# Attention and its output products: a written order of turnings, scores and half products on all engines, in place of the planner's

## The chip, the cores and the metric

The kernel runs on one core of a Trainium2 chip. The metric is the device time of one execution in microseconds. The engines are named as in the profile: PE (TensorE, matrix products; its weight loads are PEld), DVE (VectorE), ACT (ScalarE), POOL (GpSimd), and SP (SyncE), which issues the DMAs.

## The reference

One layer of a diffusion backbone for 512 latent tokens (width 1024) and 256 context tokens: a half-step SwiGLU FFN, token mixing, a second half-step SwiGLU FFN, all in float32. The part at issue is the token mixing and where the second FFN begins.

```
def one_block(q_blk):                       # 128 queries, 8 heads, 512 + 256 keys
    s = einsum('bqhd,bkhd->bhqk', q_blk, k_all) * scale
    p = softmax(s, axis=-1)
    return einsum('bhqk,bkhd->bqhd', p, v_all)

attn = block_attention(q, k_all, v_all)     # 8 heads of 64
sg   = chunk_gmlp(u, v, ...)                # 8 groups of 64
x    = x + mx[5] * (concatenate([attn, sg]) @ w_out)
x    = ffn_sublayer(x, mx[6], mx[7], mx[8], norm3_w, ffn2_w1, ffn2_w3, ffn2_w2)
```

## The kernel before, in words

**Arithmetic.** Every large product is done as three matmuls: each operand is split into a high part, rounded to the matmul's format, and a low part, the remainder (`mm3`, line 165: high·high, low·high, high·low). Making a pair takes a copy on ACT and a subtraction on DVE; `Stream.split` (line 138) does it for weights, in halves of 512 columns, after `Stream.half` has loaded a weight unit of 128 x 1024 by an SP DMA.

**Attention** (lines 1484 to 1606) has 8 heads and 4 blocks of 128 queries, so 32 steps (h, t).

- `qk_head` (1487) turns a head's queries (4 turnings) and keys (2 x 3 turnings) by matmuls with the identity, and splits them into qth, qtl, kth, ktl.
- `scores` (1509): 6 matmuls of 128 x 384 into a two-bank tile `big`, of which there are two; DVE takes the row maximum mx (1519), ACT the exponential pe with its row sum sm (1520), DVE the reciprocal (1521), and POOL scales pe (1522).
- `probs_t` (1525) turns the 6 blocks of pe in two banks `mm` of three, of which there are four; ACT copies the high part pth (1539), DVE subtracts the low part ptl (1540). The second bank of every odd block goes another way: ACT copies it to pf (1535), and POOL makes both parts (1536, 1537).
- `pv` (1542): for two blocks together, 12 matmuls of 128 x 256 by the values vv, then ol on ACT (1551), oc on DVE (1552), and the pair mixh on ACT and mixl on POOL (1554, 1555), which the output products read.
- `out_mm` (1557): output products of one 128-wide tile of the model dimension. The gate's half of w_out is multiplied ahead of and between the first scores, in 8 tiles of 12 matmuls of 128 x 512; the attention's half needs mixh and mixl, and is done for token half 0 and then half 1, in tiles of 12 matmuls of 128 x 256 each.

The step loop (1586) puts scores three steps ahead of the turnings (`LOOK`), and the four weight units of the attention's half (uo0 to uo3) at steps 4, 7, 10 and 13.

**What sets the order.** Engines run their own instructions in order. In this part `nc.ordered` is False (from line 1322): the program's order is only a hint, and a planner that works with estimated durations decides each engine's order. `Core` (62) hands out engines: with `nc.ordered = True` vector, scalar and gpsimd are wrapped in `Pinned` (51), which keeps their instructions in program order; with "all", tensor too. From line 1661 the order is pinned by True.

**After the attention.** `out_mms` (1643) and `out_evs` (1649) do the attention's half: matmuls, the addition into x on DVE, and squares of x on ACT. The sums of squares over the tiles, sqa, are added on DVE by `SsqAcc.flush` (403), one object for each token half, sA and sB (1657), which are handed `nc.vector` when they are made, before line 1661. `done` (425) sums over partitions by a matmul with ones and derives rstd on DVE (rv). `h3` (1627) then forms the second FFN's normed input, hfA into the blocks b11 and b21, hfB into b12 and b22. The second FFN starts with plain products (`plain`: 48 matmuls of 128 x 256 for two weight units and one token half) and goes on with a Winograd scheme from about 845 us on.

## Time and profile before

| | |
|---|---|
| median of 3 runs | 1152.52 us (1152.01 to 1155.87) |
| profiled execution: its own time | 1152.95 us |
| profiled execution: span of the trace | 1151.2 us |
| mean granted TensorE clock | 0.999 |
| busy: PE, DVE, ACT, POOL | 1132.2, 910.8, 534.2, 319.3 us |
| first turning of a query | 670.52 us |
| first output product of token half 1 | 782.19 us |

The profile is of one execution. A row of a timeline gives the start in us from the span's start, the duration, the engine, the line, the operation, output <- inputs by the program's names, shapes, and a count where several alike follow one another; in brackets stands how long the engine stood idle before it and what it waited for. Matmuls overlap in the array, so the distance of two starts, not the duration, is what one costs. Windows give the engines' busy time in a stretch.

### The profile page before, as it was taken

Reading aid. Unit: us, or ns where it says so; the run is one execution under the profiler, and the core shown is the slowest. Engines: PE = TensorE matmul, PEld = TensorE weight load, DVE = VectorE, ACT = ScalarE, POOL = GpSimd, SP = SyncE. Lnnn points to the kernel's source line nnn. Section 1 sums busy time; section 2 is a strip of 40 time slices with the busy share of each in tenths; the row PEclk is TensorE's granted clock in tenths of the full one; section 3 lists DMA queues with packets and bytes.
Section 4 is the critical chain, followed back from the end, with each engine's and each line's share of the span. In section 5 each row is a group of like instructions: output and inputs, shape, how many; then the busy total and the mean of one; then the engine's idle time right before and its main releaser. Section 6 shows DMA issues by size and latency. Waiting matters only on the chain. (4 is left out here: it accounts for less than half of the span.)

```text
span 1151.2 us, 18763 instructions
## 1 busy us (share of the span) xinstructions
PE 1132.2 (98%) x7084; PEld 1071.9 (93%) x7084; DVE 910.8 (79%) x1687; ACT 534.2 (46%) x1085; POOL 319.3 (28%) x277
## 2 busy tenths in 40 slices
PE   8999999999999999999999999999999999999998
PEld 6799999999999999999988788999999989898997
DVE  6978989888888788867647979869876969686884
ACT  5555421431344214445735448976543535353451
POOL 0002302311333023200027536760013425152330
PEclk9999999999999999999999999999999999999999
DMA  9530253244334664322343101002121422233312
GB/s 343 187 131 19 92 190 117 102 160 147 116 126 146 235 201 166 110 69 64 100 137 102 55 19 58 18 1 92 56 93 56 145 76 93 91 111 110 111 38 92
DMA packets 35674, 125.89 MB, mean 109 GB/s; under 512 B 3712, under 2 KB 10624, under 8 KB 30976
## 3 DMA queue, kind: packets, MB, share of 16 engines
q1 hardware_dynamic: 35440, 124.63, 31.6%
q8 instruction: 56, 0.92, 0.3%
q14 instruction: 34, 0.28, 0.1%
q10 hardware_dynamic: 144, 0.06, 0.0%
HBM read 122.58 MB, written 2.10 MB: 108 GB/s over the span
## 5 line engine op out<-in xcount | busy, mean ns | idle before, releaser
L59 POOL TENSOR_TENSOR block<-block 128x512 f32<-128x512 f32 x69 | 105.0, 1522 | 395.2 <-DVE opl L59 392.5
L59 DVE TENSOR_TENSOR opl<-block,oph 128x512 fp32r<-128x512 f32 x216 | 183.1, 854 | 32.5 <-ACT oph L59 30.2
L59 ACT CAST oph<-block 128x512 fp32r<-128x512 f32 x216 | 133.8, 621 | 142.3 <-PE mm L59 93.5
L59 PE MATMUL mm<-gh,oph 128*128 128x384 f32 (+1 forms) x440 | 155.2, 353 | 0.0
L59 PE MATMUL mm<-gl,oph 128*128 128x384 f32 (+1 forms) x440 | 154.9, 352 | 0.0
L59 PE MATMUL mm<-gh,opl 128*128 128x384 f32 (+1 forms) x440 | 154.9, 352 | 0.0
L59 DVE SCALAR_TENSOR_TENSOR x<-mm,g,x 128x256 f32<-128x256 f32 (+2 forms) x184 | 83.0, 489 | 48.9 <-PE mm L59 48.2
L59 ACT CAST oph<-raw 128x512 fp32r<-128x512 f32 x105 | 63.8, 619 | 88.7 <-PE mm L59 66.7
L59 POOL TENSOR_TENSOR block<-s,block 128x512 f32<-128x512 f32 x35 | 47.1, 1347 | 150.9 <-DVE opl L59 150.3
L59 PEld LDWEIGHTS mm<-gh,opl 128*128 128x128 f32 x440 | 82.6, 188 | 5.7
L59 PEld LDWEIGHTS mm<-gh,oph 128*128 128x128 f32 x440 | 82.6, 188 | 5.6
L59 PEld LDWEIGHTS mm<-gl,oph 128*128 128x128 f32 x440 | 82.6, 188 | 5.5
L59 DVE TENSOR_TENSOR opl<-raw,oph 128x512 fp32r<-128x512 f32 x105 | 70.4, 684 | 9.2 <-ACT oph L59 8.7
L59 PE MATMUL mm<-hh,oph 128*128 128x384 f32 x192 | 64.5, 336 | 0.0
L59 PE MATMUL mm<-hl,oph 128*128 128x384 f32 x192 | 64.2, 334 | 0.0
L59 PE MATMUL mm<-hh,opl 128*128 128x384 f32 x192 | 64.1, 334 | 0.0
L59 DVE SCALAR_TENSOR_TENSOR junk<-raw,cb 128x1024 bf16<-128x1024 f32 x48 | 62.2, 1309 | 0.0
L59 POOL TENSOR_TENSOR s<-block 128x512 f32<-128x512 f32 x34 | 50.5, 1486 | 18.9 <-DMA block<-wst 18.9
L59 PE MATMUL one<-hh,oph 128*128 128x384 f32 x144 | 48.1, 334 | 0.0
L59 PE MATMUL one<-hl,oph 128*128 128x384 f32 x144 | 48.1, 334 | 0.0
L59 PE MATMUL one<-hh,opl 128*128 128x384 f32 x144 | 48.1, 334 | 0.0
L59 DVE SCALAR_TENSOR_TENSOR raw<-raw,cb 128x1024 f32<-128x1024 f32 x32 | 42.1, 1323 | 6.2 <-DMA raw<-wada 6.1
(662 smaller groups left out, 3471.1 us busy)
## 6 DMA issues: line engine op xcount, KB each, us to landing
raw<-wst SPq DMA_DIRECT2D x77, 512.0 KB, 3.7
block<-wst SPq DMA_DIRECT2D x36, 1024.0 KB, 4.9
raw<-wada SPq DMA_DIRECT2D x56, 512.0 KB, 4.0
scale<-wada SPq DMA_DIRECT2D x8, 512.0 KB, 7.6
shift<-wada SPq DMA_DIRECT2D x8, 512.0 KB, 7.4
x<-xT SPq DMA_DIRECT2D x5, 512.0 KB, 6.7
raw<-wfirst SPq DMA_DIRECT2D x8, 256.0 KB, 7.1
out<-x SPq DMA_DIRECT2D x7, 256.0 KB, 2.3
```

The lines of the kernel that those rows point to most:

```text
L59: return lambda *a, **k: self.tc.keep_in_program_order(f(*a, **k))
```

## The change

Only the attention's part is rewritten, and one line behind it. The amount of arithmetic stays the same: the same matmuls, splits and loads.

- After the third weight unit of the gate's half, `nc.ordered = "all"`: the order of all four compute engines is the program's from here to the head of the second FFN, where True follows as before.
- Four banks are taken once and kept: A0 and A1 for turnings of probabilities (TB), Q0 for a piece of a head, P0 for the products by values. The scores keep the two tiles `big`.
- A step i = 3 to 31 is written out: maximum of step i−1, reciprocal and scaling of step i−2, the 6 turnings of step i−3, one piece of the next head (queries, keys, keys, none), the evacuation of a product by values, the high and low parts of the turnings, exponential of step i−1, 6 scores of step i, and 6 of the 12 matmuls of a product by values.
- The first two steps' scores stand between the last tiles of the gate's half. The halves of the weights uo1 to uo3 come one by one: the high half at the end of steps 6, 10, 14, 18, 22, 26, its low half ("late") in the next step behind the maximum. The two halves of uo0 come before step 3, the second one between the exponential of step 1 and the maximum of step 2.
- At the end the first four output tiles of token half 0 stand between the last turnings and products by values, their fourth heads' pair last.
- sA and sB are now made while `nc.ordered` is "all", so the `nc.vector` that they keep is the one that pins.

The core of the diff:

```diff
+    og2 = st.unit(U_OG + 2)
+    nc.ordered = "all"
+    A0, A1, Q0, P0 = (mm() for _ in range(4))
+    TB = A0, A1
...
+    s_mm(1)
+    s_mm(2)
+    s_norm(0)
...
+    uo_half(0)()
+    evac_lat(A0, 7, 1)
+    s_max(1)
+    s_exp(1)
+    uo_half(1)()
+    late = None
+    for i in range(3, LAST):
+        j = i - 3
+        if i in (3, 4, 11):
+            raw_uo.append(st.half(wst, U_OA + len(raw_uo)))
+        s_max(i - 1)
+        if late:
+            late()
+            late = None
+        s_norm(i - 2)
+        t_mm(j, TB)
+        piece = (i // 4 + 1, i % 4) if i % 4 < 3 and i // 4 + 1 < HEADS else None
+        if piece:
+            qk_mm(*piece, Q0)
+        p = (i - 7) // 2
+        if i >= 7 and i % 2:
+            pv_out(p, P0)
+        for a in range(2):
+            t_hi(j, a, TB[a])
+            t_lo(j, a, TB[a])
+        if piece:
+            qk_hi(*piece, Q0)
+            qk_lo(*piece, Q0)
+        s_exp(i - 1)
+        if i >= 7 and i % 2:
+            pv_mix(p, nc.gpsimd)
+        if i in (6, 10, 14, 18, 22, 26):
+            late = uo_half(i // 4 + 1)
+        s_mm(i)
+        if i >= 5:
+            pv_mm((i - 5) // 2, range(3) if i % 2 else range(3, 6), P0)
...
     for q in range(4):
-        out_evs(0, sA, q, out_mms(0, q))
+        out_evs(0, sA, q, early[q] if q < 2 else out_mms(0, q))
```

Here `uo_half(n)` does the high half at once and returns the low half as a function; `s_norm` is the reciprocal and POOL's scaling, `t_mm` the turnings, `t_hi` and `t_lo` their two parts, `pv_mm` and `pv_out` the product by values and its evacuation, `pv_mix` the pair for the output products.

More of the change, by code (lines that the diff above doesn't have):

```diff
@@ L1485, in layer_kernel @@
     ip = ictx.enter_context(tc.tile_pool(name="ip", bufs=2))
-    def qk_head(h):
-        qth = ip.tile([QH, 512], F32R, tag="qth", name=f"qth{h}")
-        qtl = ip.tile([QH, 512], F32R, tag="qtl", name=f"qtl{h}")
-        kth = ip.tile([QH, 768], F32R, tag="kth", name=f"kth{h}")
-        ktl = ip.tile([QH, 768], F32R, tag="ktl", name=f"ktl{h}")
-        pt = mm()
-        for t in range(4):
-            nc.tensor.transpose(pt[:QH, t * P : t * P + P], qn[:, t, h, :], ident)
-        w = wqk[:QH, 0:1]
-        nc.scalar.activation(qth, pt[:QH], AF.Copy, scale=w)
-        nc.vector.scalar_tensor_tensor(qtl, pt[:QH], w, qth.bitcast(F32), ALU.mult, ALU.subtract)
-        for a in range(2):
-            pb = mm()
-            for t in range(3):
-                nc.tensor.transpose(pb[:QH, t * P : t * P + P], kn[:, 3 * a + t, h, :], ident)
-            c = slice(384 * a, 384 * a + 384)
-            nc.scalar.copy(kth[:, c], pb[:QH, :384])
-            nc.vector.tensor_sub(ktl[:, c], pb[:QH, :384], kth[:, c].bitcast(F32))
-        return qth, qtl, kth, ktl
@@ L1507, in layer_kernel, with qk_mm @@
-    last_out = []
-    def scores(h, t, tiles):
-        qth, qtl, kth, ktl = tiles
-        pb = big()
+    heads, pes, pts, sms, ols = {}, {}, {}, {}, {}
+    steps = [(h, t) for h in range(HEADS) for t in range(4)]
+    LAST = len(steps)
+    def qk_mm(h, n, pt):
+        if n == 0:
+            heads[h] = [ip.tile([QH, c], F32R, tag=f"{s}t{p}", name=f"{s}t{p}{h}") for s, c in (("q", 512), ("k", 768)) for p in "hl"]
+            for t in range(4):
+                nc.tensor.transpose(pt[:QH, t * P : t * P + P], qn[:, t, h, :], ident)
+        else:
+            for t in range(3):
+                nc.tensor.transpose(pt[:QH, t * P : t * P + P], kn[:, 3 * n - 3 + t, h, :], ident)
@@ new lines, in qk_hi, with qk_lo @@
+    def qk_hi(h, n, pt):
+        if n == 0:
+            nc.scalar.activation(heads[h][0], pt[:QH], AF.Copy, scale=wqk[:QH, 0:1])
+        else:
+            nc.scalar.copy(heads[h][2][:, 384 * n - 384 : 384 * n], pt[:QH, :384])
+    def qk_lo(h, n, pt):
+        th, tl = heads[h][:2] if n == 0 else [t[:, 384 * n - 384 : 384 * n] for t in heads[h][2:]]
+        if n == 0:
+            nc.vector.scalar_tensor_tensor(tl, pt[:QH], wqk[:QH, 0:1], th.bitcast(F32), ALU.mult, ALU.subtract)
+        else:
+            nc.vector.tensor_sub(tl, pt[:QH, :384], th.bitcast(F32))
@@ L1512, in scores, with s_mm @@
+    def s_mm(i):
+        h, t = steps[i]
+        qth, qtl, kth, ktl = heads[h]
+        pb = sms[i] = big()
         s = slice(t * P, t * P + P)
@@ L1515, in scores, with s_max @@
             mm3(nc, pb[:, n, :384], (qth[:, s], qtl[:, s]), (kth[:, m], ktl[:, m]), True, True)
-        mx = ip.tile([P, 1], F32, tag="mx", bufs=4, name=f"mx{h}{t}")
-        sm = ip.tile([P, 1], F32, tag="sm", bufs=4, name=f"sm{h}{t}")
-        pe = ip.tile([P, 768], F32, tag="pe", bufs=4, name=f"pe{h}{t}")
+    def s_max(i):
+        pb = sms[i]
+        mx = ip.tile([P, 1], F32, tag="mx", bufs=4, name=f"mx{i}")
         nc.vector.tensor_reduce(mx, pb[:, :, :384], axis=AX.XY, op=ALU.max, negate=True)
+        sms[i] = pb, mx
@@ L1520, in scores, with s_exp, s_norm, by_pool @@
+    def s_exp(i):
+        pb, mx = sms.pop(i)
+        sm = ip.tile([P, 1], F32, tag="sm", bufs=4, name=f"sm{i}")
+        pe = ip.tile([P, 768], F32, tag="pe", bufs=4, name=f"pe{i}")
         nc.scalar.activation(pe.rearrange("p (a c) -> p a c", a=2), pb[:, :, :384], AF.Exp, bias=mx, accum_out=sm)
+        pes[i] = pe, sm
+    def s_norm(i):
+        pe, sm = pes[i]
         nc.vector.reciprocal(sm, sm)
         nc.gpsimd.tensor_scalar(pe, pe, sm, 0.0, ALU.mult, ALU.add)
-        return pe
-    def probs_t(pe, pth, ptl, c0):
-        c = slice(c0, c0 + P)
+    def by_pool(j, a):
+        return j % 2 == 1 and a == 1 and j < LAST - 4
@@ L1527, in probs_t, with t_mm @@
+    def t_mm(j, banks):
+        pe = pes.pop(j)[0]
+        if j % 2 == 0:
+            pts[j // 2] = [ip.tile([P, 6, 256], F32R, tag=f"pt{p}", name=f"pt{p}{j}") for p in "hl"]
         for a in range(2):
-            pq = mm()
             for i in range(3):
-                nc.tensor.transpose(pq[:, i * P : i * P + P], pe[:, (3 * a + i) * P : (3 * a + i) * P + P], ident)
-            src = pq[:, :384].rearrange("p (k c) -> p k c", c=P)
-            b = slice(3 * a, 3 * a + 3)
-            if c0 and a:
-                pf = ip.tile([P, 3, P], F32, tag="pf", bufs=1, name=f"pf_{nc.next_id()}")
-                nc.scalar.copy(pf, src)
-                nc.gpsimd.tensor_scalar(pth[:, b, c], pf, 1.0, 0.0, ALU.mult, ALU.add)
-                nc.gpsimd.tensor_sub(ptl[:, b, c], pf, pth[:, b, c].bitcast(F32))
-                continue
@@ L1539, in probs_t @@
-            nc.scalar.copy(pth[:, b, c], src)
-            nc.vector.tensor_sub(ptl[:, b, c], src, pth[:, b, c].bitcast(F32))
-    def pv(h, half, pth, ptl):
-        pt = mm()
-        for t in range(6):
-            nc.tensor.matmul(pt[:, :256], vv[:, t, h, :], pth[:, t, :], start=t == 0, stop=False)
-            nc.tensor.matmul(pt[:, :256], vv[:, t, h, :], ptl[:, t, :], start=False, stop=t == 5)
-        r = slice((h % 2) * 64, (h % 2) * 64 + 64)
-        c = slice(half * 256, half * 256 + 256)
-        oc = ip.tile([P, 256], F32, tag="oc", name=f"oc{h}{half}")
-        ol = ip.tile([P, 256], F32, tag="ol", bufs=1, name=f"ol{h}{half}")
+                nc.tensor.transpose(banks[a][:, i * P : i * P + P], pe[:, (3 * a + i) * P : (3 * a + i) * P + P], ident)
@@ new lines, in t_parts, with t_hi @@
+    def t_parts(j, a, bank):
+        c, b = slice(j % 2 * P, j % 2 * P + P), slice(3 * a, 3 * a + 3)
+        return bank[:, :384].rearrange("p (k c) -> p k c", c=P), [t[:, b, c] for t in pts[j // 2]]
+    def t_hi(j, a, bank):
+        src, (th, tl) = t_parts(j, a, bank)
+        if by_pool(j, a):
+            pf = ip.tile([P, 3, P], F32, tag="pf", bufs=1, name=f"pf_{j}")
+            nc.scalar.copy(pf, src)
+            nc.gpsimd.tensor_scalar(th, pf, 1.0, 0.0, ALU.mult, ALU.add)
+            nc.gpsimd.tensor_sub(tl, pf, th.bitcast(F32))
+        else:
+            nc.scalar.copy(th, src)
@@ new lines, in t_lo, with pv_mm, pv_out @@
+    def t_lo(j, a, bank):
+        if not by_pool(j, a):
+            src, (th, tl) = t_parts(j, a, bank)
+            nc.vector.tensor_sub(tl, src, th.bitcast(F32))
+    def pv_mm(p, ts, pt):
+        th, tl = pts[p]
+        for t in ts:
+            nc.tensor.matmul(pt[:, :256], vv[:, t, p // 2, :], th[:, t, :], start=t == 0, stop=False)
+            nc.tensor.matmul(pt[:, :256], vv[:, t, p // 2, :], tl[:, t, :], start=False, stop=t == 5)
+        if t == 5:
+            pts.pop(p)
+    def pv_out(p, pt):
+        r = slice((p // 2 % 2) * 64, (p // 2 % 2) * 64 + 64)
+        oc = ip.tile([P, 256], F32, tag="oc", name=f"oc{p}")
+        ol = ip.tile([P, 256], F32, tag="ol", bufs=1, name=f"ol{p}")
@@ L1551, in pv, with pv_mix @@
         nc.scalar.copy(ol[0:64], pt[64:P, :256])
         nc.vector.tensor_add(oc[r], pt[0:64, :256], ol[0:64])
-        last_out[:] = [oc]
-        nc.scalar.copy(mixh[r, h // 2, c], oc[r])
-        nc.gpsimd.tensor_sub(mixl[r, h // 2, c], oc[r], mixh[r, h // 2, c].bitcast(F32))
-    def out_mm(pt, unit, dd, c, n):
+        ols[p] = oc[r]
+    def pv_mix(p, eng):
+        r = slice((p // 2 % 2) * 64, (p // 2 % 2) * 64 + 64)
+        o = [m[r, p // 4, p % 2 * 256 : p % 2 * 256 + 256] for m in (mixh, mixl)]
+        nc.scalar.copy(o[0], ols[p])
+        eng.tensor_sub(o[1], ols.pop(p), o[0].bitcast(F32))
@@ L1558, in out_mm @@
+    def out_mm(pt, unit, dd, c, n, ks=range(4)):
         uh, ul = unit
-        for k in range(4):
+        for k in ks:
             s = slice((dd * 4 + k) * P, (dd * 4 + k) * P + P)
             mm3(nc, pt[:, :n], (uh[:, s], ul[:, s]), (mixh[:, k, c], mixl[:, k, c]), k == 0, k == 3)
-    steps = [(h, t) for h in range(HEADS) for t in range(4)]
-    LOOK = 3
-    pes, pts = {}, {}
-    def step_scores(i):
-        h, t = steps[i]
-        pes[i] = scores(h, t, heads[h])
-        if t == 1 and h + 1 < HEADS:
-            heads[h + 1] = qk_head(h + 1)
@@ L1573, in layer_kernel, with og @@
-    heads = {}
-    for q in range(4):
+    def og(q, unit, dd, pt):
+        out_mm(pt, unit, dd, slice(0, 512), 512)
+    for q in range(2):
         unit = st.unit(U_OG + q)
@@ L1577, in layer_kernel @@
             pt = mm()
-            out_mm(pt, unit, dd, slice(0, 512), 512)
+            og(q, unit, dd, pt)
             evac_lat(pt, q * 2 + dd, 1)
-        if q == 2:
-            heads[0] = qk_head(0)
-            for i in range(LOOK):
-                step_scores(i)
-    uo = []
-    for i in range(LOOK, len(steps) + LOOK + 2):
-        if i < len(steps):
-            step_scores(i)
-        if i in (4, 7, 10, 13):
-            st.pin = pin
-            uo.append(st.unit(U_OA + len(uo), oap, f"uo{len(uo)}") if len(uo) < 2 else st.unit(U_OA + len(uo)))
-            st.pin = lambda i: i
-        j = i - LOOK
-        if 0 <= j < len(steps):
-            h, t = steps[j]
-            if t % 2 == 0:
-                pts[h, t // 2] = (ip.tile([P, 6, 256], F32R, tag="pth", name=f"pth{j}"),
-                                  ip.tile([P, 6, 256], F32R, tag="ptl", name=f"ptl{j}"))
-            probs_t(pes.pop(j), *pts[h, t // 2], (t % 2) * P)
-        j = i - LOOK - 1
-        if 0 <= j < len(steps) and j % 2 == 1:
-            h, t = steps[j]
-            pv(h, t // 2, *pts.pop((h, t // 2)))
+    og2 = st.unit(U_OG + 2)
@@ new lines, in layer_kernel @@
+    nc.ordered = "all"
+    A0, A1, Q0, P0 = (mm() for _ in range(4))
+    TB = A0, A1
+    raw_og = st.half(wst, U_OG + 3)
+    raw_uo = [st.half(wst, U_OA)]
+    og(2, og2, 0, P0)
+    evac_lat(P0, 4, 1)
+    og3 = [st.operand(raw_og[:, i : i + 512]) for i in (0, 512)]
+    og3 = Halves([o[0] for o in og3]), Halves([o[1] for o in og3])
+    og(2, og2, 1, A0)
+    nc.scalar.activation(epsc2, epsc, AF.Exp)
+    qb = (Q0, A1, P0)
+    for n in range(3):
+        qk_mm(0, n, qb[n])
+        qk_hi(0, n, qb[n])
+        qk_lo(0, n, qb[n])
@@ new lines, in layer_kernel, with uo_half @@
+    evac_lat(A0, 5, 1)
+    ob = bigs(2)[0]
+    og(3, og3, 0, ob)
+    s_mm(0)
+    for n in range(3):
+        qk_mm(1, n, qb[n])
+        qk_hi(1, n, qb[n])
+    s_max(0)
+    qk_lo(1, 0, qb[0])
+    s_exp(0)
+    evac_lat(ob, 6, 1)
+    qk_lo(1, 1, qb[1])
+    og(3, og3, 1, A0)
+    qk_lo(1, 2, qb[2])
+    s_mm(1)
+    s_mm(2)
+    s_norm(0)
+    uo = [[oap.tile([P, 1024], F32R, name=f"uo{w}{p}") for p in "hl"] for w in range(2)]
+    def uo_half(n):
+        w, i = n // 2, n % 2
+        s = slice(i * 512, i * 512 + 512)
+        if w < 2:
+            dst = [t[:, s] for t in uo[w]]
+        else:
+            dst = st.pair()
+            if i == 0:
+                uo.append([])
+            uo[w].append(dst)
+        nc.scalar.copy(dst[0], raw_uo[w][:, s])
+        return lambda: nc.vector.tensor_sub(dst[1], raw_uo[w][:, s], dst[0].bitcast(F32))
@@ new lines, in layer_kernel @@
+    for w in (2, 3):
+        uo[w] = [Halves([o[e] for o in uo[w]]) for e in range(2)]
+    i = LAST
+    s_max(i - 1)
+    s_norm(i - 2)
+    t_mm(i - 3, TB)
+    for a in range(2):
+        t_hi(i - 3, a, TB[a])
+        t_lo(i - 3, a, TB[a])
+    pv_mm(13, range(3, 6), P0)
+    early = [bigs(2), TB]
+    half0 = slice(0, 256)
+    for dd in range(2):
+        out_mm(early[0][dd], uo[0], dd, half0, 256, range(3))
+    s_exp(i - 1)
+    s_norm(i - 1)
+    pv_out(13, P0)
+    t_mm(i - 2, TB)
+    Y = bigs(2)
@@ new lines, in layer_kernel @@
+    t_mm(i - 1, Y)
+    for b, banks in ((i - 2, TB), (i - 1, Y)):
+        for a in range(2):
+            t_hi(b, a, banks[a])
+            t_lo(b, a, banks[a])
+    pv_mix(13, nc.gpsimd)
+    pv_mm(14, range(6), P0)
+    pv_mm(15, range(6), Q0)
+    pv_out(14, P0)
+    pv_mix(14, nc.vector)
+    out_mm(TB[0], uo[1], 0, half0, 256, range(3))
+    for dd in range(2):
+        out_mm(early[0][dd], uo[0], dd, half0, 256, range(3, 4))
+    out_mm(TB[1], uo[1], 1, half0, 256, range(3))
+    for dd in range(2):
+        out_mm(TB[dd], uo[1], dd, half0, 256, range(3, 4))
@@ L1604, in layer_kernel @@
+    pv_out(15, Q0)
+    last_oc = ols[15]
+    pv_mix(15, nc.vector)
     kctx.close()
-    nc.scalar.activation(epsc2[64:P], last_out[0][64:P, 0:1], AF.Abs_reciprocal_sqrt, bias=epsc[64:P], scale=0.0)
+    nc.scalar.activation(epsc2[64:P], last_oc[:, 0:1], AF.Abs_reciprocal_sqrt, bias=epsc[64:P], scale=0.0)
     ictx.close()
```

## The prediction

> **What bounds the kernel now.** I began with the page's busy times.

> ```profile
> PE 1132.2 (98%) x7084; PEld 1071.9 (93%) x7084; DVE 910.8 (79%) x1687; ACT 534.2 (46%) x1085; POOL 319.3 (28%) x277
> ```

> TensorE (PE) is busy for 98% of the span, so a new order can gain only where PE stands still or where its matmuls start further apart than they must. The change concerns the stretch from the first turning of a query at 670.52 to the first output product of token half 1 at 782.19, and through a side effect the head of the second FFN. I therefore cut that stretch into windows; the columns are PE, PEld, DVE, ACT and POOL busy, granted clock, DMA share, GB/s.

> ```profile
> 670.52:690.00 19.48, 19.35 (x120) 17.37 (x119) 14.99 (x27) 13.02 (x28) 5.68 (x7) 1.00 0.00 0
> 690.00:720.00 30.00, 27.24 (x195) 25.52 (x194) 28.19 (x55) 26.22 (x61) 19.44 (x23) 1.00 0.18 58
> 720.00:760.00 40.00, 40.00 (x298) 38.63 (x297) 33.09 (x70) 36.35 (x86) 29.91 (x39) 1.00 0.03 11
> 760.00:782.19 22.19, 21.76 (x174) 20.68 (x172) 12.93 (x30) 14.28 (x34) 10.82 (x14) 1.00 0.04 10
> ```

> From 720 to 760 PE does not stop. From 690 to 720 it is idle for 2.76 us, and DVE has little room there (28.19 of 30). Busy time hides the rest, since pipelined matmuls overlap; the starts in PE's timeline show it.

> ```profile
> 679.73 0.39 PE L169 MATMUL mm<-mixl,oph 128*128 128x512 f32 x1
> ...
> 680.86 0.34 PE L168 MATMUL big<-kth,qth 96*128 96x384 f32 x1
> ...
> 682.78 0.34 PE L170 MATMUL big<-kth,qtl 96*128 96x384 f32 x1
> ...
> 685.32 0.60 PE L1494 MATMUL mm<-ident,qn 128*96 128x128 f32 x4
> 685.75 0.49 PE L1501 MATMUL mm<-ident,kn 128*96 128x128 f32 x3
> ...
> 689.52 0.28 PE L1545 MATMUL mm<-pth,vv 128*128 128x256 f32 x1
> ...
> 690.84 0.28 PE L1546 MATMUL mm<-ptl,vv 128*128 128x256 f32 x1
> 691.40 0.44 PE L168 MATMUL big<-kth,qth 96*128 96x384 f32 x1 [0.29 <-ACT pe L1520]
> ```

> Start to start: 512 wide 0.226 (five in 1.13), scores 0.1745 (eleven in 1.92), turnings 0.108 (four in 0.43), 256 wide 0.12 (eleven in 1.32). By the code this stretch holds 24 matmuls of 512 (5.4), 192 of scores (33.5), 272 turnings (80 of heads, 192 of probabilities: 29.4), and 288 of 256 (192 by values, 96 output products: 34.6): 102.9 in all. It takes 111.67. The excess, **8.8 us**, is all that a better order can win. The waits of PE from 682 to 720 name the longest stops (total, times, longest):

> ```profile
> PE mm L1530 <- DVE ptl L1540: 1.5, 1, 1.5
> PE big L168 <- ACT pe L1520: 0.9, 3, 0.4
> ```

> The 1.5 comes from DVE and POOL together, as their timelines show:

> ```profile
> 695.72 3.18 DVE L140 TENSOR_TENSOR uo1l<-raw,uo1h 128x512 fp32r<-128x512 f32 x2 [0.20 <-ACT uo1h L139]
> ```
> ```profile
> 695.16 0.74 POOL L1555 TENSOR_TENSOR mixl<-oc,mixh 64x256 fp32r<-64x256 f32 x1
> 695.86 1.01 POOL L1537 TENSOR_TENSOR ptl<-pf,pth 128x384 fp32r<-128x384 f32 x1
> 696.86 0.91 POOL L1522 TENSOR_SCALAR pe<-pe,sm 128x768 f32<-128x768 f32 x1
> ```

> Two low halves of an output weight took 3.18 where the pair at 689.15 (below) took 1.27: the 1.9 more falls together with three POOL operations in a row, and the low halves of the probabilities, which free PE's bank, stood behind them.

> **The change, part by part.**

> *Removed.* The planner's order goes, and with it the 8.8 us of excess.

> *Steady steps.* A written step is 6 turnings, 3 or 4 turnings of a head piece in three steps of four, 6 scores and 6 products by values: 0.65 + 0 to 0.43 + 1.05 + 0.72 = 2.42 to 2.85, 10.7 per head of four steps. What the other engines need comes from the groups of the whole stretch:

> ```profile
> L1519 DVE TENSOR_REDUCE mx<-big 128x1 f32<-128x768 f32 x32 | 30.3, 948 | 1.3 <-PE big L170 1.2
> L1520 ACT ACTIVATE pe<-big,mx 128x768 f32<-128x768 f32 x32 | 29.1, 911 | 4.7 <-DVE mx L1519 4.5
> L1540 DVE TENSOR_TENSOR ptl<-mm,pth 128x384 fp32r<-128x384 f32 x48 | 25.2, 548 | 3.0 <-ACT pth L1539 2.8
> L1539 ACT CAST pth<-mm 128x384 fp32r<-128x384 f32 x48 | 21.9, 483 | 2.4 <-PE mm L1530 2.2
> L1520 ACT ACTIVATION_READ_ACCUMULATOR pe<-big,mx 128x1 f32 x32 | 6.6, 205 | 0.0
> ```

> In 720 to 760, where PE sets the pace, DVE is busy 33.1 and ACT 36.4 of 40, or 8.9 and 9.7 per head of 10.7. The half weights, which came before 720, add some 0.6 to each in six heads (9.5 and 10.3); the rest of the work per head is the same, so PE stays the bound, with little room on ACT. The handover nearest to failing is the pair of turning banks: turnings end 0.65 into a step, ACT's two copies follow by about 1.5, DVE's second subtraction by 2.0, and the next turnings come at 2.42 at the earliest. That leaves some 0.4, and I count the steady stalls at nothing; without that cover 28 steps pay for each tenth (2.8 us).

> *Switches.* Each step goes once from turnings to scores and once to products by values; a first score is followed after 0.26 to 0.28 instead of 0.1745 (691.40 to 691.68 in the same timeline), against a short start after the last turning. I take 0.03 for each of 32: **+0.9**.

> *Start.* Let t be the end of score 1. Its maximum ends at t+1.05 and its exponential with the accumulator's read at t+2.2. PE does score 2 (1.05) and the first turnings (0.65) and is at score 3 at t+1.7; score 3 needs the bank of score 1: **+0.6**. Then the written order puts a half weight between that exponential and maximum 2:

> ```profile
> 695.08 1.13 ACT L139 CAST uo1h<-raw 128x512 fp32r<-128x512 f32 x2
> ```
> ```profile
> 689.15 1.27 DVE L140 TENSOR_TENSOR uo0l<-raw,uo0h 128x512 fp32r<-128x512 f32 x2
> ```

> High half t+2.2 to t+2.8, low half to t+3.5, behind it on DVE maximum 2 to t+4.4 and the two low parts of the first turnings to t+5.4. The second turnings wait for these two banks; PE has finished score 3 at t+3.35. **+2.1**, the largest single cost that I see; at best DVE reads half weight and maximum in another overlap and it is 1.

> *Late low halves.* In six later steps a low half (0.64) stands on DVE between the maximum and the reciprocal, so ahead of the low parts. Lower end 0 (the 0.4 of slack holds most of it), upper end 1.9 (what POOL made of the row at 695.72). POOL's subtraction (1.01) of the step before ends by my count within 0.3 of the maximum's end; near the lower end, 0.1 each: **+0.6**.

> [...]

> *Tail.* The interleaved output products have their banks and operands early; 0.2 for the last handover. The sum of the additions is 0.9 + 0.6 + 2.1 + 0.6 + 0.2 = 4.4, so the attention gains 8.8 − 4.4 = **4.4**.

> *Head of the second FFN.* The sums of squares sA and sB are now made while every engine is pinned, and so they keep the vector engine that pins: their additions stay where the program has them instead of being moved by the planner.

> ```profile
> 800.10 0.95 DVE L411 TENSOR_TENSOR sqa<-sqa,sq 128x256 f32<-128x256 f32 x2
> ```
> ```profile
> 801.43 2.49 DVE L59 TENSOR_TENSOR opl<-raw,oph 128x512 fp32r<-128x512 f32 x4
> ...
> 812.46 0.48 DVE L59 SCALAR_TENSOR_TENSOR b22l<-hfB,s,b22h 128x256 fp32r<-128x256 f32 x1
> ```
> ```profile
> 799.06 0.39 PE L169 MATMUL big<-b21l,w0h 128*128 128x256 f32 x1 [1.17 <-DVE b21l L59]
> ```

> By the built order sA's last two pairs both come after the last x, one pair (0.87 from issue to issue) later than now, and PE is already waiting on that chain (the 1.17 at 799.06): of it I pass 0.6 on. sB's last pair falls behind the four weight subtractions (2.49), and PE does the 34 matmuls left of plain(2,0) (4.1) before sB's sum, a plain that must itself wait for the third of those subtractions (+0.35). So rB and all of h3's second half come about 4.7 later. What covers this:

> ```profile
> 809.00:820.00 11.00, 11.00 (x94) 11.00 (x93) 9.35 (x25) 5.20 (x12) 0.00 (x0) 1.00 0.00 1
> 820.00:835.00 15.00, 15.00 (x127) 15.00 (x126) 13.13 (x32) 8.84 (x23) 0.00 (x0) 1.00 0.21 71
> 835.00:845.00 10.00, 10.00 (x86) 10.00 (x85) 8.07 (x14) 4.55 (x11) 3.82 (x3) 1.00 0.01 2
> ```
> ```profile
> L169 PE MATMUL big<-b22l,oph x8: 283/283/283, 816.9 to 819.4; 128*128 128x256 f32 x8
> ```

> PE reads the first b22l at 816.9, now written at 812.9; 4.7 later is 817.6, and PE itself is 0.95 late by then: covered, with only 0.2 to spare. DVE has 1.65 + 1.87 + 1.93 = 5.4 of idle up to 845, so the lag is nearly gone when the Winograd operands are due; 0.5 for the rest. Sum **+1.45**.

> *Total.* 1152.95 (the profiled execution's time, its span of 1151.2 and what lies around it) − 4.4 + 1.45 = 1150.0. The median shown, 1152.52, lies 0.43 under that execution; this measurement tells about 0.3%, or 3.46 us, from no change, so faster begins below 1149.06 and slower above 1155.98.

> **The rivals.**
> *Half the costs hidden.* If DVE takes the start in a kinder overlap (1 instead of 2.1) and the head's 1.45 is absorbed by the same 5.4 of idle, the attention gains 5.5 and nothing is given back: 1152.95 − 5.5 = 1147.4 at best, 1148 in the middle. For it: DVE's idle. Against it: the 1.17 shows that PE waits for DVE exactly there.
> *The gain eaten.* The 0.2 to spare at b22l doesn't hold, or steady steps lose 0.1 each: +2.5, about 1152.5. For it: the thin cover. Against it: 720 to 760 without a stop.
> *Slower: POOL holds the late low halves.* In a written order DVE can do nothing else meanwhile, so each of the six passes the wait on to the low parts and to PE. Price 1.0 (one subtraction) to 1.9 (seen) each, 6 to 11 in all: 1156 to 1161. It decides from about 1.0 each. For it: the row at 695.72. Against it: POOL's subtraction is due to end as the low half starts.
> *Not the order that it says.* The order is written on every engine and the built order follows it, so this could only be a load or a bank that comes late in all steps; that costs what the second rival costs, and I give it no time of its own.

> **How the numbers follow.** Forecast 1150.0 (1148.5 to 1152) 0.46; half hidden, 1148, 0.26; eaten, 1152.5, 0.14; POOL, 1156 and over, 0.14. Faster: the second case and a sixth of the first, 0.34. Slower: 0.14. Same: 0.52. The range leaves out the best corner and the upper half of POOL's case: 1146.5 to 1156.

> **What would show it.** Right: from 720 on, steps of 10.7 per head without idle PE; one stop of about 2 us before the second turnings, named for ptl; b21l and rv late in the FFN's head, rv near 4 to 5 us after its place now. Wrong: a stop of PE in each step (then the 0.4 of slack was misjudged), low halves of uo of 1.5 or more in the trace (POOL), or PE waiting for b12l or b22l.

## The result, and the profile after

The changed kernel takes 1156.00 us (median of 18 runs, 1153.73 to 1158.27), the kernel before 1153.36 on the same chip (18 runs). The ratio is 1.0023, with a 95% interval of 1.0014 to 1.0032: slower by 1.6 to 3.7 us. The prediction had 1150.0, faster by 2.9, and the time lies at the top end of its range. The profiled execution of the changed kernel took 1154.98 us (span 1153.2), 2.0 more than that of before.

Three marks on PE cut both spans in the same places: the first turning of a query, the last output product of half 1, and the end. First the marks in the timeline of the changed kernel, then the second one in that of before (its first one is 670.52, its end 1151.2):

```profile
669.17 0.60 PE L59 MATMUL mm<-ident,qn 128*96 128x128 f32 x4
...
793.71 0.28 PE L170 MATMUL mm<-mixh,opl 128*128 128x256 f32 x1
```
```profile
795.45 0.28 PE L170 MATMUL mm<-mixh,opl 128*128 128x256 f32 x1
```

| stretch | before | after | difference |
|---|---|---|---|
| up to the first turning | 670.5 | 669.2 | −1.4 |
| attention and output products | 124.9 | 124.5 | −0.4 |
| second FFN to the end | 355.7 | 359.5 | +3.8 |

The first row isn't the change's doing: the old execution had 3.4 us at half clock in it (649.5 to 652.9), the new one had not. The second row is the attention with the output products: it gains almost nothing where 4.4 was forecast. The third loses 3.8.

What PE waits for in these stretches of the changed kernel (total, times, longest):

```profile
PE mm L59 <- ACT p L59: 1.9, 1, 1.9
PE mm L59 <- POOL pe L59: 1.9, 1, 1.9
PE big L169 <- DVE b21l L59: 1.9, 2, 1.4
PE mm L425 <- DVE sqa L59: 1.2, 1, 1.2
PE mm L59 <- DVE oc L59: 0.5, 2, 0.3
PE big L59 <- ACT pe L59: 0.4, 1, 0.4
```

The old waits for ptl are gone. Line 59 is the wrapper through which every pinned instruction is issued, so here the tile names tell the place: pe are the second turnings of the start, sqa the sum of squares of half 0, p the first Winograd products. The windows of the changed kernel (columns as before):

```profile
686.00:689.00 3.00, 3.00 (x15) 2.87 (x13) 2.28 (x5) 2.17 (x5) 2.07 (x4) 0.50 0.00 0
690.00:720.00 30.00, 29.67 (x224) 29.02 (x223) 27.25 (x54) 27.25 (x65) 20.30 (x26) 1.00 0.05 19
720.00:760.00 40.00, 39.60 (x295) 38.62 (x294) 35.99 (x71) 36.58 (x86) 29.41 (x38) 1.00 0.08 27
782.00:803.00 21.00, 17.89 (x141) 17.03 (x141) 19.70 (x47) 11.85 (x26) 0.00 (x0) 1.00 0.25 83
```

The last of these stretches in the kernel before:

```profile
782.00:803.00 21.00, 19.50 (x155) 18.79 (x155) 20.37 (x49) 13.14 (x30) 0.00 (x0) 1.00 0.28 96
```

From 690 to 720 PE is idle for 0.3 us instead of 2.8, as intended. But from 686 to 689 its clock is halved, from 720 to 760 it now loses 0.4, and from 782 to 803 it is idle for 3.1 (before: 1.5). Three places are therefore suspected: the **start** of the written order with the half clock behind it, the **late low halves**, and the **head** of the second FFN, where nothing was rewritten.

### The profile page after: what moved, and what is told of

It is laid out like the page before. It is cut to its first block, busy times and chain, and to the rows that moved or that the text cites. A ratio compares the mean times of both kernels' runs of the same rounds, so it can differ in the third digit from the quotient of the medians.

```text
span 1153.2 us, 18842 instructions
## 1 busy us (share of the span) xinstructions
PE 1131.5 (98%) x7084; PEld 1073.8 (93%) x7084; DVE 913.1 (79%) x1691; ACT 534.0 (46%) x1086; POOL 312.9 (27%) x271
## 4 chain that ended last, share of the span: by engine, by line
PE 81%; DVE 11%; ACT 3%; issue 2%; POOL 2%; DMA 1%; DVEq 0%; ACTq 0%; POOLq 0%
PE mm L59 50%; PE one L59 17%; PE big L59 6%; DVE opl L59 2%; PE big L565 1%; PE mm L168 1%; PE mm L169 1%; PE mm L170 1%; PE mm L551 1%; DVE junk L59 1%; PE mm L318 1%; DMA raw<-wst 1%; DVE hfB L59 1%; DVE hfA L59 1%; ACT oph L59 1%
## 5 line engine op out<-in xcount | busy, mean ns | idle before, releaser
L59 POOL TENSOR_TENSOR block<-block 128x512 f32<-128x512 f32 x69 | 104.7, 1518 | 394.5 <-DVE opl L59 391.8
L59 DVE TENSOR_TENSOR opl<-block,oph 128x512 fp32r<-128x512 f32 x216 | 184.2, 859 | 31.9 <-ACT oph L59 29.7
L59 ACT CAST oph<-block 128x512 fp32r<-128x512 f32 x216 | 133.7, 621 | 143.2 <-PE mm L59 97.6
L59 PE MATMUL mm<-gh,oph 128*128 128x384 f32 (+1 forms) x440 | 155.3, 353 | 0.0
L59 PE MATMUL mm<-gl,oph 128*128 128x384 f32 (+1 forms) x440 | 155.0, 352 | 0.0
L59 PE MATMUL mm<-gh,opl 128*128 128x384 f32 (+1 forms) x440 | 154.9, 352 | 0.0
L59 DVE SCALAR_TENSOR_TENSOR x<-mm,g,x 128x256 f32<-128x256 f32 (+2 forms) x185 | 83.9, 493 | 48.9 <-PE mm L59 48.8
L59 ACT CAST oph<-raw 128x512 fp32r<-128x512 f32 x111 | 67.5, 619 | 92.7 <-PE mm L59 68.4
L59 POOL TENSOR_TENSOR block<-s,block 128x512 f32<-128x512 f32 x35 | 47.0, 1344 | 150.5 <-DVE opl L59 149.9
L59 PEld LDWEIGHTS mm<-gh,opl 128*128 128x128 f32 x440 | 82.6, 188 | 5.6
L59 PEld LDWEIGHTS mm<-gh,oph 128*128 128x128 f32 x440 | 82.6, 188 | 5.6
L59 PEld LDWEIGHTS mm<-gl,oph 128*128 128x128 f32 x440 | 82.6, 188 | 5.6
L59 DVE TENSOR_TENSOR opl<-raw,oph 128x512 fp32r<-128x512 f32 x111 | 75.6, 696 | 7.9 <-ACT oph L59 7.3
L59 PE MATMUL mm<-hh,oph 128*128 128x384 f32 x192 | 64.5, 336 | 0.0
L59 PE MATMUL mm<-hl,oph 128*128 128x384 f32 x192 | 64.2, 334 | 0.0
L59 PE MATMUL mm<-hh,opl 128*128 128x384 f32 x192 | 64.2, 334 | 0.0
L59 DVE SCALAR_TENSOR_TENSOR junk<-raw,cb 128x1024 bf16<-128x1024 f32 x48 | 62.1, 1308 | 0.2 <-DMA raw<-wada 0.2
L59 POOL TENSOR_TENSOR s<-block 128x512 f32<-128x512 f32 x34 | 50.2, 1475 | 20.1 <-DMA block<-wst 20.1
L59 DVE SCALAR_TENSOR_TENSOR raw<-raw,cb 128x1024 f32<-128x1024 f32 x32 | 42.1, 1322 | 8.1 <-DMA raw<-wada 8.0
L59 PE MATMUL one<-hh,oph 128*128 128x384 f32 x144 | 48.1, 334 | 0.0
L59 PE MATMUL one<-hl,oph 128*128 128x384 f32 x144 | 48.1, 334 | 0.0
L59 PE MATMUL one<-hh,opl 128*128 128x384 f32 x144 | 48.1, 334 | 0.0
```

The lines of the kernel that those rows point to most:

```text
L59: return lambda *a, **k: self.tc.keep_in_program_order(f(*a, **k))
```

## The experiments

All are compared with the kernel before, run on the same chip beside them. Its median was 1154.23 for the first four runs below the changed kernel and 1154.67 for the last four, which ran on another chip. The ratio is worked out from all runs, and so isn't quite the quotient of the two medians.

| kernel | median us | ratio to before, 95% interval |
|---|---|---|
| changed kernel | 1156.00 | 1.0023 (1.0014 to 1.0032) |
| sums free | 1153.03 | 0.9989 (0.9977 to 1.0001) |
| before, sums pinned | 1159.12 | 1.0039 (1.0023 to 1.0054) |
| start mended | 1154.42 | 1.0002 (0.9992 to 1.0013) |
| low halves moved | 1154.41 | 1.0009 (0.9996 to 1.0021) |
| flush early | 1153.48 | 0.9989 (0.9980 to 0.9997) |
| all three | 1149.63 | 0.9958 (0.9946 to 0.9969) |
| all three, flush in place of free sums | 1149.85 | 0.9960 (0.9949 to 0.9972) |
| start mended, a stop put in | 1155.13 | 1.0002 (0.9991 to 1.0013) |

**The sums of squares free again.**

```diff
-    sA, sB = SsqAcc(t3, 256, nc.vector), SsqAcc(t3, 256, nc.vector)
+    sA, sB = SsqAcc(t3, 256, tc.nc.vector), SsqAcc(t3, 256, tc.nc.vector)
```

> The changed kernel, with the two sums of squares sA and sB handed the vector engine that does not pin, as in the kernel before; the attention is untouched. Theory H (the pinned sums make the head of the second FFN late, 0.9 us at b21l and 2.8 at the start of the Winograd products): those two terms go, 3.7 us, so 1156.0 - 3.7 = 1152.3, ratio to before about 0.999, and the wait of PE for p near 847 is gone. Rival S (the loss is the stop at the start of the attention and the half clock after it, which no run forced into the head): the time stays at 1155.5 to 1156, and PE is late by as much again in another place.

Measured: 0.9989, so 0.0034 or 3.9 us under the changed kernel. Theory H holds. The waits of PE from the first turning to 860 us in this kernel:

```profile
PE mm L59 <- POOL pe L59: 1.9, 1, 1.9
PE big L169 <- DVE b21l L59: 1.2, 1, 1.2
PE mm L425 <- DVE sqa L411: 0.8, 1, 0.8
PE mm L59 <- DVE oc L59: 0.5, 2, 0.3
PE big L59 <- ACT pe L59: 0.4, 1, 0.4
```

The wait for p is gone and b21l is back at the 1.2 of before, while the attention's waits (pe, oc) stand where they stood.

**The side effect alone, in the kernel before.**

```diff
-    sA, sB = SsqAcc(t3, 256, nc.vector), SsqAcc(t3, 256, nc.vector)
+    sA, sB = SsqAcc(t3, 256, nc.pinned["vector"]), SsqAcc(t3, 256, nc.pinned["vector"])
```

> The kernel before, with only sA and sB handed the pinned vector engine: the side effect alone, without the new attention. Theory H: slower by what e1 wins back, 2.8 to 3.7 us, so 1153.4 + 3 = 1156.2 to 1157.1, with rv of half 1 some 3 to 5 us later and PE waiting 1.9 us near 845. Rival S: no change that can be told from 1153.4.

Measured: 1.0039, 4.5 us slower, a little over the expected 2.8 to 3.7, whose upper end lies in the interval (2.7 to 6.2). Two of this kernel's waits of PE:

```profile
PE mm L59 <- ACT p L59: 2.0, 1, 2.0
PE big L169 <- DVE b21l L59: 1.9, 2, 1.4
```

They are those of the changed kernel, with the old attention ahead of them. The second half's rv comes at 807.92, 12.9 us behind the last output product, where the kernel before has 8.4 (803.84): 4.5 later, as expected. So the loss in the head belongs to the pinned sums, not to the new order of the attention.

**The flush of sB ahead of the weight subtractions, sums still pinned.**

```diff
+    sB.flush()
     us.append(up_units(2, U_UP2))
     plain(0, 0)
-    sB.flush()
     rB = sB.done()
```

> The changed kernel, sums still pinned, but the last pair of sB's sum is added ahead of the four weight subtractions (the flush stands before the load of the third weight unit). Theory H in its narrow form (of the head's loss, what counts is that sB's last pair stands behind those four subtractions and PE's plain products, so that rv of half 1 comes 2.8 late and DVE never makes it up): rv comes back to its place, the wait for p near 847 goes, 2.8 us faster than the changed kernel, ratio to before 0.9995 to 1.0005; sA's 0.9 stays. Rival (DVE's other work in the head is what is late, the sum of squares only stands next to it): less than 1 us, ratio 1.0015 or more.

Measured: 0.9989, 3.9 us, above the 2.8 expected (its 0.9995 lies in the interval); the narrow form of theory H holds, and PE's wait for p is gone. DVE's timeline in this kernel, then in the changed one, and there the sum's matmul on PE:

```profile
800.98 0.88 DVE L59 TENSOR_TENSOR sqa<-sqa,sq 128x256 f32<-128x256 f32 x2
801.77 2.49 DVE L59 TENSOR_TENSOR opl<-raw,oph 128x512 fp32r<-128x512 f32 x4
804.18 0.42 DVE L59 SCALAR_TENSOR_TENSOR rv<-mm,ri 128x256 f32<-128x256 f32 x1
```
```profile
799.73 2.49 DVE L59 TENSOR_TENSOR opl<-raw,oph 128x512 fp32r<-128x512 f32 x4
802.14 0.87 DVE L59 TENSOR_TENSOR sqa<-sqa,sq 128x256 f32<-128x256 f32 x2
806.62 0.42 DVE L59 SCALAR_TENSOR_TENSOR rv<-mm,ri 128x256 f32<-128x256 f32 x1 [3.61 <-ACT ri L59]
```
```profile
805.48 0.59 PE L425 MATMUL mm<-sqa,ones 128*128 128x256 f32 x2
```

Two additions, 0.87 together, moved by one place. Behind the four subtractions they end at 803.0, and then DVE stands for 3.6 us, because in PE's built order the rest of plain(2,0) comes ahead of the sum's matmul, which starts at 805.5; rv follows at 806.6. sA's waits (b21l 1.9, sqa 1.2) still stand in this kernel, yet it gains as much as the one with free sums; so the runs don't show that sA's late pair costs the 0.9 in the end.

**The start mended.**

```diff
     s_exp(1)
-    uo_half(1)()
     late = None
...
             t_lo(j, a, TB[a])
+        if i == 3:
+            uo_half(1)()
```

> The changed kernel, with the second half of uo0 moved from between the exponential of step 1 and the maximum of step 2 to behind the low parts of the first turnings (step 3). Theory S: the stop of 1.91 us before the second turnings shrinks to 0.3 or less, and the window of half clock that follows it (1.6 us in the profile) is gone in most executions: 1.6 to 3.2 us faster than the changed kernel, 1152.8 to 1154.4, and the share of executions with a second window of half clock falls. Rival (the half clock comes by chance, wherever PE stands): 1.6 only, and the granted clock is spread as before.

Measured: 1.0002, so 0.0021 or 2.4 us under the changed kernel. The stop of 1.91 is gone. What is left is a wait at the third turnings, a little over the 0.3 expected (PE's timeline):

```profile
687.84 0.87 PE L59 MATMUL mm<-ident,pe 128*128 128x128 f32 x6 [0.40 <-POOL pe L59]
```

The time alone doesn't tell the theory from the rival's 1.6: by the two intervals the difference is 0.8 to 4.0. The half clock speaks for the theory, but less simply than expected. This profile has none behind the start; nor have two of the four profiles that keep the stop (sums free and low halves moved have none, the changed kernel and flush early have one). Over the runs, 5 of these 12 had a granted clock of 1.000 over the whole span. Of the 53 runs of the four kernels that keep the stop 7 had it, none of them among the changed kernel's 18; of the 23 runs of the three versions with the start mended and no other stop put in, 9 had it. The last section has the places of the stops that had a window behind them, and of those that had none.

**The late low halves moved.**

```diff
         s_max(i - 1)
-        if late:
-            late()
-            late = None
         s_norm(i - 2)
...
             qk_lo(*piece, Q0)
+        if late:
+            late()
+            late = None
         s_exp(i - 1)
```

> The changed kernel, with the late low halves moved from behind the maximum to behind the low parts of the step's turnings on DVE. Theory L (each of the six holds oc, and with it the bank of the products by values, for 0.24 to 0.42 us): the waits for oc go, 1.5 to 2 us faster than the changed kernel, so 1154.0 to 1154.5. [...]

Measured: 1.0009, 1.6 us under the changed kernel, as theory L has it; by the two intervals alone it could also be nothing. (By the medians it is 2.4: four of the 12 runs had a granted clock of 0.995 or 0.996, which none of the changed kernel's had, and they carry the ratio up.) The profile decides: the half weights' low halves, in the changed kernel and here (duration least, median, most in ns; first and last start):

```profile
L59 DVE TENSOR_TENSOR uo1l<-raw,uo1h x2: 693/820/946, 694.2 to 705.0; 128x512 fp32r<-128x512 f32 x2
```
```profile
L59 DVE TENSOR_TENSOR uo1l<-raw,uo1h x2: 682/682/683, 695.0 to 705.8; 128x512 fp32r<-128x512 f32 x2
```

In the changed kernel the second one starts at 704.99, beside POOL's subtraction of 704.38 (1.01 long), and takes 0.95; behind it comes oc, whose bank the next product by values needs. At the later place, 705.76, POOL is idle (its timeline has nothing from 705.1 to 706.6), the two of uo1 take 0.68 each, and PE's waits for oc are gone. DVE now stands for 0.37 ahead of oc at 704.32, a wait put down to POOL's subtraction of 703.24 (1.00 long), and PE has no wait behind it. What these rows show is that the second low half took 0.27 more beside POOL's subtraction than with POOL idle.

**All three.** The edits of the sums, the start and the low halves together.

> The changed kernel with all three: sums free, second half of uo0 behind the first low parts, late low halves behind the low parts. If the three causes are separate places, their gains add: 3.9 + 2.4 + 1.6 = 7.9 us from the changed kernel's ratio of 1.0023, so a ratio to before of 0.9955, about 1149 where before takes 1154.2, and faster than both kernels. If they share one hidden bound (an earlier PE only waits at the next place), 4 to 5 us, ratio 0.998.

Measured: 0.9958 (forecast from the single gains: 0.9955). The gains add, so these are three separate places. Beyond the free sums alone (0.9989), the start and the low halves together bring 3.6 us, which is clear of noise where the low halves by themselves aren't. This version is faster than both kernels, by 4.9 us than the one before (interval 3.6 to 6.2). Its windows:

```profile
690.00:760.00 70.00, 69.91 (x529) 69.70 (x528) 62.70 (x128) 65.54 (x154) 51.46 (x65) 1.00 0.08 24
845.00:855.00 10.00, 10.00 (x66) 9.12 (x65) 7.44 (x15) 4.42 (x9) 0.00 (x0) 1.00 0.58 211
```

PE is idle for 0.09 us in 70 of the attention, and no longer at 845.

> The same with the sums pinned and sB's flush early instead of the sums free: 0.9 us slower than the version with free sums if only sA's last pair then still costs, ratio to before 0.9963; 3 us slower if the pinned order costs elsewhere too.

Measured: 0.9960. Between the two mended heads there is no difference that five rounds can tell; the expected 0.9 for sA is within the error.

**A stop put in by hand.** It computes the same, since x is multiplied by 1.

```diff
+        if i == 17:
+            for _ in range(4):
+                nc.vector.tensor_scalar(x[:, 0, :], x[:, 0, :], 1.0, 0.0, ALU.mult, ALU.add)
         s_max(i - 1)
```

> The changed kernel with the start mended (second half of uo0 later), and a stop of PE put in by hand in the middle of the attention: four operations on DVE ahead of the maximum in step 17, which multiply a part of x by 1 in place. They hold DVE for about 2.4 us, of which some 0.4 are slack: PE stops about 2 us. If a stop of that length brings a window of half clock wherever it stands, the time rises by 2 + 1.7, so 3.7 us over the kernel with the start mended (ratio 1.0002), ratio 1.0034, few executions keep a clock of 1.0, and the profile shows 3.4 us at half clock right behind the stop. If the window at the start had nothing to do with the stop, 2 us, ratio 1.002, and the clocks are spread as without the stop.

Measured: 1.0002, no difference from the start mended without the stop: as a time, a miss for both readings. The profile shows why. The stop is there, and the half clock behind it; first PE's timeline, then a window:

```profile
724.20 0.38 PE L59 MATMUL mm<-pth,vv 128*128 128x256 f32 x1 [2.06 <-DVE oc L59]
```
```profile
725.50:728.00 2.50, 2.50 (x12) 2.47 (x11) 1.78 (x5) 1.77 (x4) 1.74 (x3) 0.50 0.00 0
```

But in this kernel the planner, which still orders PE in the head, places sB's sum further forward: DVE waits 2.05 us for it instead of 3.60, PE's wait for p falls from 2.0 to 0.6, and the head is 2.1 us shorter (358.2 from the last output product to the end, against 360.3). The stop and its half clock cost 4.3 us from the first turning to the last output product (125.2 against 120.9); by the sum of both the time should still rise by some 2 in a run where the window comes, and by some 0.5 in one where it doesn't (by an estimate a window costs 1.7, half of its 3.4 at a clock of 0.50). The two intervals together (1.8 either way) hardly allow the first for every run. It doesn't come in every run: 2 of the 11 kept a clock of 1.000. So that a window of half clock can follow such a stop is shown in this profile. The clocks of the runs only lean that way (6 of 11 at 0.997, against 3 of 12 without the stop, on another chip), and the price in the median isn't shown.

## Why the prediction was wrong

*Removed, and steady steps: right.* The new order keeps PE busy: 29.67 of 30 where it was 27.24, and 69.91 of 70 in the version with all three repairs. There the attention is 5.9 us shorter than before up to the first output product of half 1. (The excess that I started from is 8.5 and not 8.8: 782.19 is the third matmul of half 1, its first starts at 781.95.) The slack of 0.4 at the turning banks held, and ACT and DVE are not the bound.

*Start: right in size and place, not in the operation.* Forecast 0.6 + 2.1; the profile has waits of 0.38 and 1.91. The second is put down to POOL's pe, not to ptl as I wrote, since I left the reciprocal and POOL's scaling out of the chain: maximum 2 ends at 683.2, the reciprocal and POOL's scaling behind it at 684.4, ptl at 684.2. Both hang on the same low half, and moving it took the stop away.

*The half clock behind it: left out.* The old profile had 3.4 us at a granted clock of 0.5 behind stops of PE, and I gave it no term and no rival. The changed kernel has such a window from 685.9 to 689.4, right behind the 1.91, where the same matmuls cost 1.6 more by their starts. By the starts of PE, the attention gains 1.3 up to half 1's first output product, 2.9 without this window, of the 4.4 forecast; sA's late pair then takes 0.9 back before half 1's last one (the wait of 1.2 for sqa).

*Late low halves: place right, size too small.* I took 0.1 each, near the lower end, and the sum +0.6. Five of the six put off a product by values by 0.24 to 0.42, 1.6 in sum, and the mended kernel is 1.6 faster. The rival had POOL hold each of the six for 1.0 to 1.9. In the changed kernel these five start 0.40 to 0.57 before POOL's subtraction (1.01) is over and take 0.94 to 1.11; the first of the six, which starts when it is over, takes 0.69. So they took 0.25 to 0.42 more, and the price was about a quarter of the rival's lowest, 6 in all.

*Head of the second FFN: the step that failed by most.* That sums pinned in order make rv late was right (2.8 later in absolute time, 4.5 measured from the last output product, forecast 4.7), and so was b21l with what follows up to the first b12 (0.9, forecast 0.95). The step that failed reads "DVE has 1.65 + 1.87 + 1.93 = 5.4 of idle up to 845, so the lag is nearly gone". It isn't. DVE's timeline before, then in the changed kernel:

```profile
838.66 0.41 DVE L59 TENSOR_TENSOR sl<-mm,sl 128x256 f32<-128x256 f32 x1
...
843.01 0.42 DVE L59 TENSOR_TENSOR sl<-mm,sl 128x256 f32<-128x256 f32 x1 [0.80 <-ACT sl L59]
```
```profile
841.50 0.41 DVE L59 TENSOR_TENSOR sl<-mm,sl 128x256 f32<-128x256 f32 x1
...
844.87 0.42 DVE L59 TENSOR_TENSOR sl<-mm,sl 128x256 f32<-128x256 f32 x1
```

sl is late by 2.8 at 841.5 and still by 1.9 at 844.87, when the Winograd products have begun. ACT waits for it (1.65 us ahead of gh, before 0.49) and so makes p 1.8 later; PE, by then 0.8 ahead of its old place, waits for p. ACT, then PE, in the changed kernel:

```profile
845.32 0.40 ACT L59 CAST gh<-sl 128x256 fp32r<-128x256 f32 x1 [1.65 <-DVE sl L59]
...
846.67 0.36 ACT L59 COPY p<-mm 128x256 f32<-128x256 f32 x1
```
```profile
847.08 0.39 PE L59 MATMUL mm<-b21h,oph 128*128 128x256 f32 x1 [1.95 <-ACT p L59]
```

Of DVE's 5.4 of idle time only the 0.9 by which the lag shrank, from 2.8 to 1.9, was a reserve. Most of it (3.3 of the 5.4) stands inside chains that go from DVE to ACT and back: seven times gl waits 0.47 for ACT's gh, and these waits move along with the lag. I summed the gaps of an engine without asking which of them a late engine could skip. Sized by the experiments, the pinned sums cost 3.9 (changed kernel) or 4.5 us (kernel before), where I had 1.45.

*In sum:* forecast −4.4 + 1.45 = −2.9; by the single repairs the change costs 3.9 in the head, 2.4 at the start and 1.6 in the low halves over a new order that by itself is 4.9 faster than before. That gives +3.0, where the measurement has +2.65 (1.6 to 3.7). Between forecast and result lie 5.6 us. The head accounts for some 2.5 of them (3.9 for 1.45); the rest is the attention, by the profile 1.6 of half clock, which the sum didn't have, and 1.0 of late low halves above all. The head alone would have made it −0.5, the attention alone +0.2; it took both to make the change slower.

## What to carry to other kernels

An object that is handed an engine while a mode is set keeps that mode, so moving the line at which a pin begins can reorder code over a hundred microseconds further on: compare the built order behind the rewritten part too. Idle time of an engine in pinned order absorbs a delay only where it isn't a wait inside a chain that the delay itself carries along (here 0.9 of DVE's 5.4 us); take the gaps one by one, by releaser. In a hand-written order each extra instruction belongs behind the one that the bound engine waits for next, and each repair here is one line changed, or moved by a few places.

## What the runs showed of the hardware

Some stops of PE of about 2 us had 3.4 us at a granted clock of 0.50 behind them: 685.9 to 689.4 behind the 1.91 in the changed kernel, 725.0 to 728.4 behind the 2.06 put in by hand. Others had none: behind the 1.95 us at 845 the changed kernel's profile has none, and the 1.93 at the start of the kernel with free sums has none either.

```profile
682.53:685.94 3.41, 1.50 (x13) 1.50 (x13) 3.03 (x7) 1.91 (x5) 1.59 (x2) 1.00 0.49 154
685.94:689.36 3.42, 3.42 (x15) 3.29 (x15) 2.62 (x6) 2.43 (x5) 2.49 (x4) 0.50 0.00 0
```
```profile
684.62:688.03 3.41, 1.56 (x13) 1.56 (x14) 3.03 (x7) 1.97 (x5) 1.65 (x2) 1.00 0.51 154
688.03:691.44 3.41, 3.41 (x26) 3.23 (x25) 2.94 (x7) 3.41 (x8) 2.57 (x4) 1.00 0.00 0
```
```profile
680.18:683.59 3.41, 2.31 (x14) 1.71 (x13) 1.84 (x5) 2.26 (x5) 0.00 (x0) 1.00 0.00 0
683.59:687.00 3.41, 2.21 (x17) 2.17 (x17) 2.56 (x8) 2.61 (x6) 2.30 (x3) 1.00 0.55 154
```

So in the changed kernel, where practically all of the stop of 1.9 lies in one stretch, a window came behind it; with free sums, where 0.08 of it lies ahead of the border, and with the low halves moved none came.

Over whole runs, the kernel before was granted a clock of 1.000 in 18 of 29 runs of the first set and in 9 of 23 of the second, the changed kernel in 0 of 18, with 0.997 in 9 of them; and those 9 runs average 1157.0 us, against 1155.4 for the 9 others. The two profiles with two such windows have a clock of 0.997 over the span, the two without any 1.000. So by its profile the changed kernel's stop cost nearly twice its length (1.9, and 1.6 by the starts for the window), and by an estimate from these clocks a part of the spread between runs of one kernel goes with the number of such windows.
